# A third, short Strassen step over k-tiles 8 and 9 of the gate/up chunk pairs, separate weight rings and sums, and a later split of p

## The chip, the cores and the metric

The kernel runs on one core of a Trainium2 chip. The metric is the time of one execution on the device in microseconds, the median of several. The engines are called as the profile calls them: PE (TensorE matmul) and PEld (its weight loads), DVE (VectorE), ACT (ScalarE), POOL (GpSimd), SP (SyncE, which issues the DMAs).

## The reference

One decoder layer on 256 tokens of width 2048, all in fp32: a half-step feed-forward network (FFN), a mixer (a gated short convolution and a gated linear recurrence), a second half-step FFN, and a gated embedding. The part that matters here is the FFN, which occurs twice with weights of 2048 x 11008 and 5504 x 2048:

```python
def swiglu(x, w_in, w_out):
    a, u = jnp.split(x @ w_in, 2, axis=-1)
    return (jax.nn.silu(a) * u) @ w_out

x = layer_norm(ALPHA * x + 0.5 * swiglu(x, ffn1_w_in[i], ffn1_w_out[i]), ln_g[i, 0], ln_b[i, 0])
...
x = layer_norm(ALPHA * x + 0.5 * swiglu(x, ffn2_w_in[i], ffn2_w_out[i]), ln_g[i, 2], ln_b[i, 2])
ple = jax.nn.sigmoid(x @ ple_w_gate[i]) * (p[i] @ ple_w_proj[i])
x = layer_norm(ALPHA * x + ple, ln_g[i, 3], ln_b[i, 3])
```

## The kernel before

**Products.** The 256 tokens are two token tiles of 128 (`t` = 0, 1). Each matrix product takes a 128 x 128 block of x as the stationary operand and 512 columns of a weight row block as the moving one. To keep fp32 accuracy, each operand is split into a high part (fp32r, a cast) and a low part (what the cast lost), and each product is three matmuls, high x high, high x low, low x high (`passes`, L962 to L964). A k-tile is 128 rows of the contracted dimension; the FFN's input product has 16.

**Weight pieces.** The whole kernel works through one list of weight pieces (`plan`). A piece is usually two k-tiles by 512 columns: 128 x 1024 numbers in SBUF. For each, SP issues a load into a buffer (`weight_dma`, L868), ScalarE casts it to the high part `wh` (`weight_cast`, L897), VectorE subtracts to get the low part `wl` (`weight_split`, L908), and then PE uses it. There are six `wh`/`wl` pairs in the FFN's main ring (`NMAIN`), and four `raw` load buffers (`NRAW`). When PE's program has passed the last use of a piece, `consumed` makes its pair free, and `feed` issues what can be issued: loads first, then a cast, then a split. Two pieces at most are cast ahead of the split.

**Ticks.** Work that belongs beside the matmuls (transposes, layer norm pieces, operand splits) is put off by a number of ticks (`defer`); a tick passes with each pair of k-tiles on PE (`tick`).

**Chunk pairs.** Each FFN has 11 column chunks of its hidden width. From the third on (nine chunks per FFN) a gate chunk and an up chunk are computed together in a `Quad`. With the two token tiles as the rows of a 2 x 2 block matrix and gate and up as the columns of another, two groups of k-tiles, "low" and "high", form a 2 x 2 by 2 x 2 product. Strassen's scheme (in Winograd's form) needs 7 products for it in place of 8, and sums of the weights (t1 to t4) and of the operands (s1 to s4). Before, k-tiles 0 to 3 are low and 4 to 7 are high: two steps of two low and two high k-tiles each. K-tiles 8 to 15 are plain: four pieces of gate (a) and four of up (u), each used for both token tiles; the up pieces use the difference d of the token tiles for one of them. The seven sums of products are accumulated in seven PSUM banks, p1 to p7, and combined on VectorE by nine instructions per quad (`after`, recorded at L425, the silu ones on ScalarE at L447 and L453).

The order of pieces in a step is "11 u0 t1 u1 22 t3 a0 t2 a1 21 t4", with 11, 12, 21 and 22 the four weight blocks of the step. These blocks are loaded into five shared buffers `sraw` (`NSRAW`), in the order 12, 22, 21, 11; each buffer is reused in turn. A weight sum is an in-place VectorE addition just ahead of the cast (L891). The same five buffers first hold the fp32 operands that the sums s1 to s4 and d are made of (`sums`), in six deferred tasks when chunk 1 begins.

**Units around it.** Each quad is followed by two units of the output product of the part before (`out_unit`, 8 k-tiles each), whose results VectorE adds to x (L485). In the second FFN, x of the layer norm before it gets its gain and offset late (`affine_rows`, L359 to L365), through `raw` buffers.

**p.** The 256 columns of p are loaded at the start (`small_loads`), transposed, split into high and low, and held to the end, where a short product uses them.

## Time and profile before

| | us |
|---|---|
| median of 3 runs (2227.93 to 2230.04) | 2228.63 |
| the profiled execution, its own time | 2228.56 |
| its span, first to last instruction | 2226.70 |

The granted clock of the profiled execution was 0.997 on average. In the rows of the profile a group has its line, engine, operation, output and inputs, form and count, then its busy time in us, the mean of one in ns, and the engine's idle time before it with what ended it. Rows of the timeline have start and duration in us. Records of matmuls overlap: a matmul's duration is longer than the step to the next one. The first FFN takes about the first 700 us, the mixer and the merge the next 700, the second FFN the next 700, and the gated embedding the rest.

### The profile page before, as it was taken

Reading aid. Unit: us, or ns where it says so; the run is one execution under the profiler, and the core shown is the slowest. Engines: PE = TensorE matmul, PEld = TensorE weight load, DVE = VectorE, ACT = ScalarE, POOL = GpSimd, SP = SyncE. Lnnn points to the kernel's source line nnn. Section 1 sums busy time; section 2 is a strip of 40 time slices with the busy share of each in tenths; the row PEclk is TensorE's granted clock in tenths of the full one; section 3 lists DMA queues with packets and bytes.
Section 4 is the critical chain, followed back from the end, with each engine's and each line's share of the span. In section 5 each row is a group of like instructions: output and inputs, shape, how many; then the busy total and the mean of one; then the engine's idle time right before and its main releaser. Section 6 shows DMA issues by size and latency. Waiting matters only on the chain.

```text
span 2226.7 us, 26935 instructions
## 1 busy us (share of the span) xinstructions
PE 2203.0 (99%) x10110; PEld 1837.0 (82%) x10110; DVE 1685.6 (76%) x1952; ACT 1127.8 (51%) x1324; POOL 10.0 (0%) x32
## 2 busy tenths in 40 slices
PE   9999999999999999999999999999999999999997
PEld 7988888888887888888888888798888888888876
DVE  6788888888885678557555875769888888888668
ACT  5555555555555534434444443645555555555463
POOL 1000000000000000000000000000000000000000
PEclk9999999999999999999999999999999999999999
DMA  7666676566653665554555665567666556666564
GB/s 255 215 204 194 198 217 202 183 192 190 207 194 128 194 200 172 174 167 152 189 190 189 199 194 192 181 200 226 209 214 197 181 185 214 200 191 192 172 218 151
DMA packets 225334, 429.98 MB, mean 193 GB/s; under 512 B 13740, under 2 KB 22452, under 8 KB 225204
## 3 DMA queue, kind: packets, MB, share of 16 engines
q1 hardware_dynamic: 225204, 428.27, 60.6%
q8 instruction: 79, 1.29, 0.2%
q14 instruction: 51, 0.42, 0.1%
HBM read 426.12 MB, written 2.10 MB: 192 GB/s over the span
## 4 chain that ended last, share of the span: by engine, by line
PE 92%; DVE 4%; DMA 2%; ACT 1%; issue 1%; SPq 0%; DVEq 0%; ACTq 0%
PE bank L962 30%; PE bank L964 29%; PE bank L963 29%; DVE wl L908 2%; PE bank L243 2%; PE bank L600 1%; DVE sraw L891 1%; DMA raw<-in_ffn_w_in_dram 1%; ACT wh L897 0%; DMA sraw<-in_ffn_w_in_dram 0%; DMA gb<-in_ln_g_dram 0%; DMA x<-in_x_dram 0%; DMA raw<-in_ffn_w_out_dram 0%; DVE x L400 0%; DVE x L401 0%
## 5 line engine op out<-in xcount | busy, mean ns | idle before, releaser
L908 DVE TENSOR_TENSOR wl<-raw,wh 128x1024 fp32r<-128x1024 f32 (+2 forms) x660 | 788.6, 1203 | 262.8 <-ACT wh L897 245.4
L897 ACT CAST wh<-raw 128x1024 fp32r<-128x1024 f32 (+2 forms) x660 | 680.4, 1035 | 581.5 <-PE bank L964 410.1
L964 PE MATMUL bank<-wh,xl 128*128 128x512 f32 (+1 forms) x1736 | 670.9, 387 | 0.7 <-DVE xl L254 0.7
L963 PE MATMUL bank<-wl,xh 128*128 128x512 f32 (+1 forms) x1736 | 671.0, 387 | 0.0
L962 PE MATMUL bank<-wh,xh 128*128 128x512 f32 (+1 forms) x1736 | 669.6, 388 | 1.3 <-ACT xh L253 0.9
L897 ACT CAST wh<-sraw 128x1024 fp32r<-128x1024 f32 x252 | 262.5, 1050 | 273.1 <-PE bank L964 120.3
L908 DVE TENSOR_TENSOR wl<-sraw,wh 128x1024 fp32r<-128x1024 f32 x252 | 306.1, 1223 | 102.5 <-ACT wh L897 98.8
L964 PEld LDWEIGHTS bank<-wh,xl 128*128 128x128 f32 x1736 | 327.0, 188 | 64.5 <-DVE xl L254 2.4
L962 PEld LDWEIGHTS bank<-wh,xh 128*128 128x128 f32 x1736 | 327.1, 188 | 63.9 <-ACT xh L253 1.7
L963 PEld LDWEIGHTS bank<-wl,xh 128*128 128x128 f32 x1736 | 327.0, 188 | 61.8 <-DVE wl L908 0.2
L963 PE MATMUL bank<-wl,gh 128*128 128x512 f32 x880 | 343.9, 391 | 0.0
L964 PE MATMUL bank<-wh,gl 128*128 128x512 f32 x880 | 342.9, 391 | 0.0
L962 PE MATMUL bank<-wh,gh 128*128 128x512 f32 x880 | 341.9, 392 | 0.0
L964 PEld LDWEIGHTS bank<-wh,gl 128*128 128x128 f32 x880 | 165.4, 188 | 34.1
L962 PEld LDWEIGHTS bank<-wh,gh 128*128 128x128 f32 x880 | 165.3, 188 | 33.8
L963 PEld LDWEIGHTS bank<-wl,gh 128*128 128x128 f32 x880 | 165.4, 188 | 33.4
L891 DVE TENSOR_TENSOR sraw<-sraw 128x1024 f32<-128x1024 f32 x144 | 175.8, 1221 | 0.7
L964 PE MATMUL bank<-wh,sl 128*128 128x512 f32 x432 | 168.5, 390 | 0.0
L963 PE MATMUL bank<-wl,sh 128*128 128x512 f32 x432 | 168.4, 390 | 0.0
L962 PE MATMUL bank<-wh,sh 128*128 128x512 f32 x432 | 164.9, 390 | 0.5 <-ACT wh L897 0.5
L962 PEld LDWEIGHTS bank<-wh,sh 128*128 128x128 f32 x432 | 81.1, 188 | 17.9 <-ACT wh L897 1.4
L963 PEld LDWEIGHTS bank<-wl,sh 128*128 128x128 f32 x432 | 81.1, 188 | 16.9
(181 smaller groups left out, 1145.8 us busy)
## 6 DMA issues: line engine op xcount, KB each, us to landing
raw<-in_ffn_w_in_dram SPq DMA_DIRECT2D x176, 512.0 KB, 4.5
raw<-in_mix_w_in_dram SPq DMA_DIRECT2D x176, 512.0 KB, 4.6
raw<-in_ffn_w_out_dram SPq DMA_DIRECT2D x168, 512.0 KB, 4.9
sraw<-in_ffn_w_in_dram SPq DMA_DIRECT2D x144, 512.0 KB, 4.7
raw<-in_mix_w_out_dram SPq DMA_DIRECT2D x32, 512.0 KB, 5.4
raw<-in_ple_w_gate_dram SPq DMA_DIRECT2D x32, 512.0 KB, 4.9
raw<-in_ffn_w_in_dram SPq DMA_DIRECT2D x32, 384.0 KB, 4.0
raw<-in_branch_w_conv_dram SPq DMA_DIRECT2D x16, 512.0 KB, 4.9
```

Of the source, the lines that this page charges most:

```text
L243: state["turned"] = nc.tensor.transpose(tp[:, i * P : (i + 1) * P], src[:, i * P : (i + 1) * P], ident).ins
L600: nc.tensor.matmul(gp[:, (h * 2 + t) * 64 : (h * 2 + t + 1) * 64], kd[:, h, t * P : (t + 1) * P], qd[:, h, t, :], start=True, stop=True)
L891: nc.vector.tensor_tensor(out=raw[:, :n, :w], in0=raw[:, :n, :w], in1=raws[el["add"]][:, :n, :w], op=ALU.add)
L897: nc.scalar.copy(h[:, :n, :w], raw[:, :n, :w])
L908: nc.vector.tensor_tensor(out=l[:, :n, :w], in0=raw[:, :n, :w], in1=h[:, :n, :w].bitcast(F32), op=ALU.subtract)
L962: nc.tensor.matmul(acc, sh, wh[:, a, :n], start=first, stop=False)
L963: nc.tensor.matmul(acc, sh, wl[:, a, :n], start=False, stop=False)
L964: nc.tensor.matmul(acc, sl, wh[:, a, :n], start=False, stop=last)
```

## The change

- K-tiles 8 and 9 become a short Strassen step of one low and one high k-tile, four pieces (h1 to h4) at the head of the quad. The tile `one` holds the step's blocks 11 and 22, the tile `three` its blocks 12 and 21, each loaded in two halves. h1 is `one`; h2 is `one` plus a repeated block 12, written to a buffer of ring "12" (t1 and t3); h3 is t2 and block 21; h4 is t4, half a piece. K-tiles 10 to 15 remain plain: three a and three u pieces. A quad has 24 pieces where it had 22.
- The short step's operand sums are made of the third chunk of operands, in `short_sums` and `made_short`; with a marker task there are ten deferred tasks where there were six, and the low sums are formed in one task.
- The five shared buffers become four rings with their own counts (`HIGH`): two for "11", one each for "12", "21", "22". A quad's ring "12" takes loads only once its h2 is made. `feed` tries the rings in a fixed order, ahead of `raw`.
- A weight sum is issued by itself (`weight_add`), ahead of casts, once what it overwrites has been split (`behind`), up to one piece ahead of the split.
- The accumulators are combined as they are complete, no longer by the name of the piece; the instructions are the same.
- p is loaded, transposed and split when the last output units of the second FFN begin (`p_operand`).

The diff's core, without blank lines and without the functions whose content only moved:

```diff
+HIGH = {"11": 2, "12": 1, "21": 1, "22": 1}
...
-NSRAW = 5
...
+    STEPS = (((0, 1), (4, 5)), ((2, 3), (6, 7)))
+    SHORT = (8, 9)
+    PLAIN = ((10, 11), (12, 13), (14, 15))
+    ORDER = ("h1 u0 h2 h3 a0 h4 11.0 u1 t1.0 22.0 t3.0 a1 t2.0 21.0 t4.0 "
+             "11.1 u2 t1.1 22.1 t3.1 a2 t2.1 21.1 t4.1").split()
     def __init__(self, stat, w, cols, width, after):
         self.stat, self.w, self.cols, self.width, self.after = stat, w, cols, width, after
-        self.els = []
-        for s in range(2):
-            lo, hi = (2 * s, 2 * s + 1), (4 + 2 * s, 5 + 2 * s)
-            n0, n1 = (8 + 4 * s, 9 + 4 * s), (10 + 4 * s, 11 + 4 * s)
+        self.shorted = False
+        made = {}
+        for s, (lo, hi) in enumerate(self.STEPS):
+            sums = (2 * s, 2 * s + 1)
             k11, k12, k21, k22 = ((self, s, n) for n in ("11", "12", "21", "22"))
             step = {
-                "11": dict(src=k11, use=[("p1", 0, lo)]),
-                "t1": dict(src=k11, add=k12, use=[("p5", "s1", lo)]),
-                "22": dict(src=k22, use=[("p3", "s4", lo)]),
-                "t3": dict(src=k12, add=k22, use=[("p7", "s3", lo)], free=[k12]),
-                "t2": dict(src=k11, add=k22, use=[("p6", "s2", lo)], drop=[k22]),
+                "11": dict(src=k11, use=[("p1", 0, lo)], load=[(k11, lo, 0), (k22, hi, 1), (k12, lo, 1), (k21, hi, 0)]),
+                "t1": dict(src=k11, add=(k11, k12), behind="11", use=[("p5", "s1", sums)]),
+                "22": dict(src=k22, use=[("p3", "s4", sums)]),
+                "t3": dict(src=k12, add=(k12, k22), behind="t1", use=[("p7", "s3", sums)], free=[k12]),
+                "t2": dict(src=k11, add=(k11, k22), behind="t1 22", use=[("p6", "s2", sums)], drop=[k22]),
                 "21": dict(src=k21, use=[("p2", 0, hi)]),
-                "t4": dict(src=k11, add=k21, use=[("p4", 1, hi)], drop=[k21], free=[k11]),
+                "t4": dict(src=k11, add=(k11, k21), behind="t2 21", use=[("p4", 1, hi)], drop=[k21], free=[k11]),
             }
-            for n, ks in (("a0", n0), ("a1", n1)):
-                step[n] = dict(load=[(ks, 0)], use=[("p2", 0, ks), ("p4", 1, ks)])
-            for n, ks in (("u0", n0), ("u1", n1)):
-                step[n] = dict(load=[(ks, 1)], use=[("p3", "d", ks), ("p5", 1, ks)])
-            step["11"]["sums"] = [(k12, lo, 1), (k22, hi, 1), (k21, hi, 0), (k11, lo, 0)]
-            order = "11 u0 t1 u1 22 t3 a0 t2 a1 21 t4".split()
-            for n in order:
-                self.els.append(dict(step[n], name=n, step=s))
+            for n, el in step.items():
+                if "behind" in el:
+                    el["behind"] = max(self.ORDER.index(f"{m}.{s}") for m in el["behind"].split())
+                made[f"{n}.{s}"] = el
+        lo, hi = self.SHORT
+        one, two, three = (self, "h", "11"), (self, "h", "12"), (self, "h", "21")
+        made["h1"] = dict(src=one, use=[("p1", 0, (lo,)), ("p3", "s4", (4,))],
+                          load=[(one, (lo,), 0), (one, (hi,), 1), (three, (lo,), 1), (three, (hi,), 0)])
+        made["h2"] = dict(src=two, add=(one, three), short="h2", behind=-1, free=[two],
+                          use=[("p5", "s1", (4,)), ("p7", "s3", (4,))])
+        made["h3"] = dict(src=three, add=(two, one), short="h3", behind=self.ORDER.index("h1"), drop=[one],
+                          use=[("p6", "s2", (4,)), ("p2", 0, (hi,))])
+        made["h4"] = dict(src=three, add=(three, three), short="h4", behind=self.ORDER.index("h3"), free=[three],
+                          n=1, use=[("p4", 1, (hi,))])
+        for i, ks in enumerate(self.PLAIN):
+            made[f"a{i}"] = dict(load=[(None, ks, 0)], use=[("p2", 0, ks), ("p4", 1, ks)])
+            made[f"u{i}"] = dict(load=[(None, ks, 1)], use=[("p3", "d", ks), ("p5", 1, ks)])
+        self.els = [made[n] for n in self.ORDER]
...
+    def high(part, name):
+        return region["high"].tile([P, KG, CC], F32, tag="b" + part, name=name, bufs=HIGH[part])
...
+        def four(x11, x12, x21, x22, s1, s2, s3, s4):
+            both(s3, x11, x21, ALU.subtract)
+            both(s1, x21, x22, ALU.subtract)
+            both(s2, s1, x11, ALU.subtract)
+            both(s4, x12, s2, ALU.add)
...
+        short = spare[:, 1, :]
+        def short_sums():
+            y = [hi[t][:, 0, i * P : (i + 1) * P] for t in range(NT) for i in range(2)]
+            four(*y, *(short[:, i * P : (i + 1) * P] for i in range(4)))
+        def made_short():
+            halves(stat, "short", 0, short, 4, "s")
+            h, l = stat.parts["short", 0]
+            for i in range(4):
+                stat.parts[f"s{i + 1}", 1] = h[:, i : i + 1, :], l[:, i : i + 1, :]
         def delta(c):
+            d = hi[0][:, c % 2, :]
+            both(d, d, hi[1][:, c % 2, :], ALU.subtract)
+            halves(stat, "d", c, d, 4, "s")
+        todo = (low_sums, lambda: made("s1", x[2]), lambda: made("s2", x[0]), lambda: made("s3", s3),
+                lambda: made("s4", x[1]), short_sums, made_short, lambda: delta(2), lambda: delta(3),
+                lambda: held.update(on=True))
+        for i, fn in enumerate(todo):
...
+                after = deque([(("p1",), first), (("p3", "p5"), second), (("p6", "p7"), third),
+                               (("p2",), fourth), (("p4",), fifth)])
...
+    def p_operand():
+        for t in range(NT):
+            pin = st.tile([P, CC], F32, tag="h", name="pin", bufs=3)
+            nc.sync.dma_start(pin[:, :256], p[0, 0, t * P : (t + 1) * P, :])
+            defer(8 + t, lambda t=t, pin=pin: to_stat(pst, t, 0, pin, 2, "g"))
...
+            base = len(plan)
             for el in u.els:
-                for key, ks, n in el.get("sums", ()):
-                    loads["sraw"].append((key, kind, u.w, ks[0] * P, 2, u.cols[n], u.width))
-                if "load" in el:
-                    (ks, n), = el["load"]
-                    el["src"] = len(plan)
-                    el["free"] = [len(plan)]
-                    loads["raw"].append((len(plan), kind, u.w, ks[0] * P, 2, u.cols[n], u.width))
-                plan.append(dict(el, n=2, w=u.width, where="main"))
+                if "add" in el:
+                    adds.append(len(plan))
+                    el["behind"] += base
+                for key, ks, n in el.get("load", ()):
+                    ring = key[2] if key else "raw"
+                    if not key:
+                        key = el["src"] = len(plan)
+                        el["free"] = [key]
+                    loads[ring].append((key, kind, u.w, ks[0] * P, len(ks), u.cols[n], u.width))
+                plan.append(dict(dict(n=2, w=u.width, where="main"), **el))
...
     def weight_dma(ring="raw"):
         key, _, w, r0, n, col, width = loads[ring].popleft()
+        at = 0
         if ring == "raw":
             raw = rp.tile([P, KG, CC], F32, tag="raw", name="raw", bufs=NRAW)
             used["raw"] += 1
+        elif key in half:
+            raw, at = half.pop(key), 1
         else:
-            raw = high("sraw")
+            raw = high(ring, "raw" + ring)
+            held[ring] += 1
+            if n == 1:
+                half[key] = raw
         src = w[r0 : r0 + n * P, col : col + width].rearrange("(a p) c -> p a c", p=P)
-        nc.sync.dma_start(raw[:, :n, :width], src)
-        raws[key] = raw
+        nc.sync.dma_start(raw[:, at : at + n, :width], src)
+        if key not in half:
+            raws[key] = raw
...
+        key, kind = loads[ring][0][:2]
+        if ring == "12" and not key[0].shorted:
+            return False
+        return kind == region["kind"] and held["on"] and (held[ring] < HIGH[ring] or key in half)
...
+    def weight_add():
+        el = plan[adds.popleft()]
+        a, b = (raws[key] for key in el["add"])
+        short = el.get("short")
+        if short == "h2":
+            out = raws[el["src"]] = high("12", "raw12")
+            held["12"] += 1
+            el["src"][0].shorted = True
+            b = b[:, 0:1, :].to_broadcast([P, 2, CC])
+        elif short == "h3":
+            out, a, b = raws[el["src"]][:, 0, :], a[:, 0, :], b[:, 1, :]
+        elif short == "h4":
+            out = a = a[:, 0, :]
+            b = b[:, 1, :]
+        else:
+            out = a
+        nc.vector.tensor_tensor(out=out, in0=a, in1=b, op=ALU.add)
+        drop(el.get("drop", ()))
+        el["added"] = True
+    def addable():
+        if not adds:
+            return False
+        i = adds[0]
+        el = plan[i]
+        if i > cur["split"] + 1 or cur["split"] <= el["behind"] or any(key not in raws for key in el["add"]):
+            return False
+        return el.get("short") != "h2" or held["12"] < HIGH["12"]
...
-        if "add" in el:
-            nc.vector.tensor_tensor(out=raw[:, :n, :w], in0=raw[:, :n, :w], in1=raws[el["add"]][:, :n, :w], op=ALU.add)
-            drop(el.get("drop", ()))
...
     def feed():
         while True:
-            if may_load("sraw"):
-                weight_dma("sraw")
-            elif may_load("raw"):
-                weight_dma()
+            ring = next((r for r in ("11", "22", "12", "21", "raw") if may_load(r)), None)
+            if ring:
+                weight_dma(ring)
+            elif addable():
+                weight_add()
             elif castable():
                 weight_cast()
...
-            for bank, t, ks in el["use"]:
+            for i, (bank, t, ks) in enumerate(el["use"]):
                 tick()
                 first = bank not in ps
                 if first:
                     ps[bank] = ptile("a", bank)
                 for a, k in enumerate(ks):
                     left[bank] -= 1
-                    passes(ps[bank], u.stat, t, k, gi, a, first and a == 0, left[bank] == 0)
+                    passes(ps[bank], u.stat, t, k, gi, a if len(ks) > 1 else i, first and a == 0, left[bank] == 0)
             consumed(gi)
-            u.after(el, ps)
+            while u.after and all(b in left and not left[b] for b in u.after[0][0]):
+                u.after.popleft()[1](ps)
...
```

More of the change, by code (lines that the diff above doesn't have):

```diff
@@ L289, in sums @@
     def sums(stat):
-        x1, x2, d = plain[0, 0], plain[1, 0], high("s3")
-        x11, x12, x21, x22, s3 = x1[:, 0, :], x1[:, 1, :], x2[:, 0, :], x2[:, 1, :], d[:, 0, :]
-        s1, s2, s4 = x21, x11, x12
-        def made(key, g, src):
-            halves(stat, key, g, src, 4, "s")
-        def third():
-            difference(x11, x21, s3)
-            made("s3", 0, s3)
-        def first():
-            difference(x21, x22, s1)
-            made("s1", 0, s1)
-        def second():
-            difference(s1, x11, s2)
-            made("s2", 0, s2)
@@ L309, in fourth, with both @@
-        def fourth():
-            nc.vector.tensor_tensor(out=s4, in0=x12, in1=s2, op=ALU.add)
-            made("s4", 0, s4)
-        def delta(c):
-            a = plain[0, 1][:, c % 2, :]
-            difference(a, plain[1, 1][:, c % 2, :], a)
-            made("d", c, a)
-            if c == 3:
-                held["freed"] += 5
-        for i, fn in enumerate((third, first, second, fourth, lambda: delta(2), lambda: delta(3))):
+        def both(o, a, b, op):
+            nc.vector.tensor_tensor(out=o, in0=a, in1=b, op=op)
@@ new lines, in four, with low_sums @@
+        def four(x11, x12, x21, x22, s1, s2, s3, s4):
[3 more added lines that the diff above has]
+            both(s4, x12, s2, ALU.add)
+        lo, hi, spare = [plain[t, 0] for t in range(NT)], [plain[t, 1] for t in range(NT)], high("11", "s")
+        x = [lo[0][:, 0, :], lo[0][:, 1, :], lo[1][:, 0, :], lo[1][:, 1, :]]
+        s3 = spare[:, 0, :]
+        def low_sums():
+            four(*x, x[2], x[0], s3, x[1])
@@ new lines, in first, with second, third @@
+                def first(ps):
+                    made["c11"] = work("h")
+                    nc.scalar.copy(made["c11"], ps["p1"])
+                def second(ps):
+                    c = made["c12"] = work("silu")
+                    nc.scalar.copy(c, ps["p3"])
+                    both(c, c, ps["p5"], ALU.add)
+                def third(ps):
+                    e = made["e"] = work("silu")
+                    made["c22"] = work("h")
+                    both(e, made["c11"], ps["p6"], ALU.add)
+                    both(made["c12"], made["c12"], e, ALU.subtract)
+                    both(e, e, ps["p7"], ALU.add)
+                    both(made["c22"], ps["p5"], e, ALU.subtract)
@@ L523, in small_loads @@
         nc.sync.dma_start(normw, hg_norm_w.broadcast_to([P, P]))
-        pin = [st.tile([P, CC], F32, tag="h", name="pin", bufs=3) for t in range(NT)]
-        for t in range(NT):
-            nc.sync.dma_start(pin[t][:, :256], p[0, 0, t * P : (t + 1) * P, :])
         def place():
@@ L531, in place @@
             nc.vector.tensor_copy(gbT, tp[:, :96])
[L532 to L542 removed]
+        defer(8, place)
+    pst = Stat()
+    def p_operand():
[3 more added lines that the diff above has]
+            defer(8 + t, lambda t=t, pin=pin: to_stat(pst, t, 0, pin, 2, "g"))
     def small_inputs():
@@ L832, in hybrid_layer @@
     plan = []
-    loads = {"raw": deque(), "sraw": deque()}
+    adds = deque()
+    loads = {ring: deque() for ring in ("raw", *HIGH)}
     for u in units:
@@ L854, in hybrid_layer @@
                 plan.append(dict(src=i, free=[i], n=len(ks), w=u.width, where=where))
-    raws, pairs = {}, {}
+    raws, pairs, half = {}, {}, {}
     cur = {"cast": 0, "split": 0}
-    used = {"raw": 0, "sraw": 0}
+    used = {"raw": 0}
     room = dict(EXTRA, main=NMAIN)
@@ L875, in may_load @@
             return used["raw"] < NRAW
-        return loads[ring][0][1] == region["kind"] and 5 <= held["freed"] and held["sraw"] - held["freed"] < NSRAW
+        key, kind = loads[ring][0][:2]
+        if ring == "12" and not key[0].shorted:
+            return False
+        return kind == region["kind"] and held["on"] and (held[ring] < HIGH[ring] or key in half)
     def drop(keys):
@@ L916, in castable @@
         el = plan[i]
-        return (el["src"] in raws and el.get("add", el["src"]) in raws and room[el["where"]]
+        return (el["src"] in raws and ("add" not in el or el.get("added")) and room[el["where"]]
                 and el["where"] in ("main", region["kind"]))
```

68 lines of the change are left out of this document (19 added, 49 removed).

## The prediction

> **What bounds the kernel now.** I read the engine totals first, then the chain that ended last.
>
> ```profile
> span 2226.7 us, 26935 instructions
> PE 2203.0 (99%) x10110; PEld 1837.0 (82%) x10110; DVE 1685.6 (76%) x1952; ACT 1127.8 (51%) x1324; POOL 10.0 (0%) x32
> ...
> PE 92%; DVE 4%; DMA 2%; ACT 1%; issue 1%; SPq 0%; DVEq 0%; ACTq 0%
> ```
>
> PE is busy almost always and carries 92% of the chain. Since matmul records overlap, I check in the timeline of PE whether they follow each other at an even step. These are the first and the last of 26 wide matmuls:
>
> ```profile
> 500.10 0.39 PE L962 MATMUL bank<-wh,xh 128*128 128x512 f32 x1
> ...
> 505.77 0.39 PE L963 MATMUL bank<-wl,xh 128*128 128x512 f32 x1
> ```
>
> 25 steps in 5.67 us are 0.2268 us each. This is the price of a matmul on the path, not the 0.39 us of its record. Second, I ask whether PE waits anywhere in the chunk pairs ("quads" below). The view of waits from 1490 to 1610 us, the stretch where VectorE is latest, has one line for PE:
>
> ```profile
> PE bank L962 <- ACT wh L897: 0.5, 2, 0.3
> ```
>
> So PE sets the time in the quads, and fewer matmuls are worth their step each. The question is how near VectorE is behind it. One quad with its two out units, by windows (PE, PEld, DVE, ACT, POOL busy, clock, DMA share, GB/s):
>
> ```profile
> 1683.00:1746.50 63.50, 63.50 (x285) 52.61 (x284) 53.67 (x53) 34.20 (x36) 0.00 (x0) 1.00 0.64 199
> ```
>
> VectorE is busy for 53.67 of 63.50 us, 85%, at full clock. That is close enough for the added sums to matter.
>
> **What is removed: matmuls.** A "product" is one k-tile for one token tile or sum, three matmuls (high x high, high x low, low x high). Before, a quad has two steps of 7 x 2 products and 8 plain pieces of 4: 28 + 32 = 60 products, 180 matmuls. After, it has the two steps (28), a short step (h1, h2 and h3 of 2 products, h4 of 1: 7) and 6 plain pieces (24): 59 products, 177 matmuls. Nine quads in each of two FFNs: 18 x 3 = 54 matmuls, 54 x 0.2268 = **-12.25 us**. All are on PE's path.
>
> The Trainium skill ("TensorE: Matmul & The Clock Gate", Part 1) gives 215.7 ns from start to start for 512 columns at the full clock. By that the saving would be an estimated 11.65 us; the trace has 226.8 ns at granted clock 1.00, so the measured step stands.
>
> **What is added: VectorE work.** Its step, from these rows of the timeline:
>
> ```profile
> 1700.00 1.23 DVE L908 TENSOR_TENSOR wl<-sraw,wh 128x1024 fp32r<-128x1024 f32 x1 [3.56 <-ACT wh L897]
> 1701.14 1.22 DVE L908 TENSOR_TENSOR wl<-raw,wh 128x1024 fp32r<-128x1024 f32 x1
> ...
> 1720.83 0.68 DVE L425 TENSOR_TENSOR silu<-h,bank 128x512 f32<-128x512 f32 x1
> 1721.43 1.22 DVE L908 TENSOR_TENSOR wl<-raw,wh 128x1024 fp32r<-128x1024 f32 x1
> ```
>
> Instructions begin 1.14 us after a wide one and 0.60 us after one of 512 columns. Before, the weights of a quad cost 22 splits and 8 adds: 30 x 1.14 = 34.20 us. After: 23 whole splits and h4's half, 26.82; 9 whole adds (h2's is new) and two of 512 columns (h3, h4), 11.46; together 38.28 us, **+4.08 us per quad**. The epilogue has the same nine instructions, after the same pieces. h2's add reads a repeated operand; nearest are a product with a repeated operand and a sum without, and they cost the same, so I charge nothing extra:
>
> ```profile
> L694 DVE TENSOR_TENSOR sg<-sg,normw 128x512 f32<-128x512 f32 x4 | 2.8, 688 | 7.5 <-ACT sg L692 7.5
> L365 DVE TENSOR_TENSOR x<-x,gb 128x512 f32<-128x512 f32 x24 | 15.6, 687 | 1.1 <-DMA gb<-in_ln_b_dram 1.1
> ```
>
> If the repetition doubled it, each quad would have 1.14 us more. ScalarE gains 1.5 casts per quad and is busy 34.20 of 63.50 us: free.
>
> **What pays for it: a DMA wait.** The five shared sraw buffers give step 1's "11" no buffer until step 0 releases one. VectorE (1700.00 above, idle 3.56 us) waits for a cast, and the cast for the load:
>
> ```profile
> 1698.92 1.05 ACT L897 CAST wh<-sraw 128x1024 fp32r<-128x1024 f32 x1 [3.74 <-DMA sraw<-in_ffn_w_in_dram]
> ...
> ACT wh L897 <- DMA sraw<-in_ffn_w_in_dram: 68.7, 16, 4.8
> ...
> 1510.78 4.57 DMA sraw<-in_ffn_w_in_dram
> ```
>
> 68.7 us in 16 waits are 4.29 us, about one per quad; the last row is one on the chain. After, ring "11" has two buffers: the short step's tile is dropped at h3's add, so 11.1 loads some ten pieces before its use. The wait goes. VectorE's time through a quad's weights was 34.20 + 4.29 = 38.49 us and becomes 38.28 us: the same. What could be late next is 12.0, since ring "12" has one buffer, which holds h2's sum until h2's split. Then VectorE still has h3 (0.60 + 1.14), a0 (1.14), h4 (0.60 + 0.60), 11.0 and u1 (2 x 1.14) ahead of the add that needs 12.0: 6.36 us, against this landing:
>
> ```profile
> sraw<-in_ffn_w_in_dram SPq DMA_DIRECT2D x144, 512.0 KB, 4.7
> ...
> gb<-in_ln_b_dram SPq DMA_DIRECT2D x16, 256.0 KB, 5.3
> ```
>
> The two half loads for each short tile (256 KB, four per quad in place of two whole loads, SP's only extra issues) land in 5.3 us or less; they are issued a quad's out units ahead. I take 0 for both.
>
> **How much VectorE may be late.** Each quad's tightest piece is t1 of step 1, right behind that wait. The end of its split against PE's first use of the low part (L963), in quad 4 of the first FFN, and quads 5, 2 and 3 of the second:
>
> ```profile
> 235.92 1.23 DVE L908 TENSOR_TENSOR wl<-sraw,wh 128x1024 fp32r<-128x1024 f32 x1
> 239.57 0.39 PE L963 MATMUL bank<-wl,sh 128*128 128x512 f32 x1
> ...
> 1704.69 1.23 DVE L908 TENSOR_TENSOR wl<-sraw,wh 128x1024 fp32r<-128x1024 f32 x1
> 1709.30 0.39 PE L963 MATMUL bank<-wl,sh 128*128 128x512 f32 x1
> ...
> 1521.22 1.23 DVE L908 TENSOR_TENSOR wl<-sraw,wh 128x1024 fp32r<-128x1024 f32 x1
> 1522.95 0.39 PE L963 MATMUL bank<-wl,sh 128*128 128x512 f32 x1
> ...
> 1583.53 1.22 DVE L908 TENSOR_TENSOR wl<-sraw,wh 128x1024 fp32r<-128x1024 f32 x1
> 1584.83 0.47 PE L963 MATMUL bank<-wl,sh 128*128 128x512 f32 x1
> ```
>
> Slack: 2.42, 3.38, 0.50 and 0.08 us. The first two stand for the 16 settled quads, the last two are the tight ones behind the layer norm. After, a quad takes PE 3 x 0.2268 = 0.68 us less and VectorE 0.21 us less, so slack shrinks by 0.47 us plus any wait W that is left. With W = 0 the settled quads keep 1.9 us or more: cost 0. The tight two would lose 0 and 0.39 us: +0.4.
>
> **The rest.** Each FFN forms short sums: four VectorE sums of 128 columns and one more 512-column cast and split. Nearest to the small sums is
>
> ```profile
> L726 DVE SCALAR_TENSOR_TENSOR cT<-uT,cw,cT 128x128 f32<-128x128 f32 x32 | 9.4, 349 | 0.0
> ...
> 1479.83 1.29 DVE L364 TENSOR_TENSOR x<-x,gb 128x512 f32<-128x512 f32 x2 [3.82 <-DMA gb<-in_ln_g_dram]
> ```
>
> which bounds them: 4 x 0.35 + 0.60 = 2.0 us, and 0 if hidden. In the second FFN they come shortly before an idle of 3.82 us on VectorE, which would absorb them; if that cover is gone, 2.0. I take +0.3. The weight rings open eight ticks later (19, not 11, of the 32 in chunk 1's units), still 13 ticks ahead of q2: 0. The seven accumulators are opened within 12 products (8.2 us), not 20. The last bank of the out units is read by VectorE after quad 6 has begun:
>
> ```profile
> 1747.91 0.39 PE L962 MATMUL bank<-wh,xh 128*128 128x512 f32 x1
> ...
> 1749.93 0.68 DVE L485 TENSOR_TENSOR x<-x,bank 128x512 f32<-128x512 f32 x1
> ```
>
> 1749.93 + 0.68 - 1747.91 = 2.7 us, in time for 8.2: 0. The p rows move from the start to the last out units: the same two loads, four transposes (0.8 us of records), casts and splits. At the start they may give back up to 0.8 us; at the end the out units need VectorE little. Their loads stand in SP's queue behind "h" buffers, ahead of weight loads with time in hand. I take 0.
>
> **Sum**, against the profiled execution's own 2228.56 us (span 2226.7; the three runs have median 2228.63): 2228.56 - 12.25 + 0.4 + 0.3 = **2217.0 us**. Its own range: down to 2214 (the 0.5 us of PE waits and p's 0.8 gone, 2215.0, and a run's scatter of 1), up to 2220 (short sums bare, both tight quads 0.5 late).
>
> **Rivals.**
> - **Slower: 12.0 comes late.** If VectorE's order puts t1.0's add right behind h2's split, nothing covers the load, and a wait W stays in every quad. A settled quad stalls by W + 0.47 - 2.9 (middle of 2.42 and 3.38), a tight one by W + 0.47 - 0.3. It decides from W = 2.8, where 18 W - 38.5 eats the 12.25 us; at 4.29 it costs 38.7: 2255 us. For it: one buffer, and 1.7 us of margin. Against: 6.36 us of other work in between. Chance 0.10.
> - **VectorE already sets the pace.** Then 18 x 4.08 = 73.4 us are added, 68.7 us of waits go, the matmuls count nothing: 2233.3 us. The even step of PE and the slack speak against it. The Trainium skill ("Perfetto Trace Analysis", Identifying the Most-Contended Engine) would rank this way: matmul busy is no measure, weight loads and VectorE occupancy are. In the windows row these are 83% and 85%, so VectorE leads by that rule. Chance 0.05.
> - **No change: the tight quads pay in full.** If in q2 and q3 of the second FFN another load (raw, gb) takes the place of the wait that goes, both lose 4.08, and the short sums 2.0: 10.2 us back, 2226.5 us. For it: slack 0.08 and the idle for gb. Against: the waits on the chain there are sraw's. Chance 0.13.
>
> **How the numbers follow.** The forecast has 0.72, all of it faster by more than 0.2% (4.5 us, about what a measurement of this kernel can tell from no change: below 2224.1). The third rival is the "same" case, 0.13. The first two are slower, 0.15. The range 2214 to 2228 holds the forecast and the third rival with a run's scatter, 0.85.
>
> **What would show it.** PE should have 54 instructions fewer (10056), with the same step. DVE should rise by about 18 x 4.08 + 4 = 77 us. The casts' wait for loads of "11" should vanish, and no wait for a "12" load above 2.8 us appear; PE's waits between 1490 and 1610 us should stay about 1 us. The forecast is wrong if PE's busy share falls in the quads, or if VectorE idles in front of the t adds.

## The result and the profile after

The changed kernel is slower: a median of 2233.86 us (2233.20 to 2236.82) against 2228.62 us (2227.02 to 2230.04), a ratio of 1.0026 [1.0016, 1.0036]. The prediction, 2217.0 us with a range up to 2228, missed by 16.9 us, and on the wrong side.

The totals of the profile after, and the engines' shares of its chain:

```profile
span 2232.4 us, 27107 instructions
...
PE 2198.4 (98%) x10056; PEld 1828.0 (82%) x10056; DVE 1761.9 (79%) x2052; ACT 1158.5 (52%) x1361; POOL 10.1 (0%) x32
...
PE 91%; DVE 5%; issue 1%; DMA 1%; ACT 1%; SPq 0%; DVEq 0%; ACTq 0%
```

The planned sizes are all there: 54 matmuls fewer, and VectorE busy for 76.3 us more (77 predicted). The span is 5.7 us longer all the same. To see where, I took all rows of PE's timeline and summed, from each matmul's start to the next, what exceeds its step (0.2268 us for 512 columns, in proportion for fewer). Below, such an excess is called a gap; a slow clock counts in it too. Some 700 matmuls of 128 columns and fewer have steps of about 0.11 us, so the totals depend on how these are counted. Strictly in proportion the whole kernels have 76.7 and 94.6 us; with 0.06 us as the least step, and without excesses under 0.05 us, they have 44.3 and 61.5, near the table's totals. Differences between kernels and the rows for the quads agree within 1.3 us in all these counts.

| gaps of PE, us | before | after |
|---|---|---|
| whole kernel | 46.2 | 63.3 |
| 100 to 160 us (quad 2, first FFN) | 0.3 | 4.4 |
| 1490 to 1620 us (quads 2 and 3, second FFN) | 1.7 | 14.5 |
| the rest | 44.2 | 44.4 |

So 12.25 us of matmuls went as planned, and 17.1 us of gaps came, nearly all of them in three of the 18 quads, the first ones of each FFN. The other 15 have no single gap above 0.3 us. The waits of PE after, first from 120 to 140 us, then from 1490 to 1610 us (us in total, times, longest):

```profile
PE bank L1030 <- DVE wl L974: 2.0, 1, 2.0
```

```profile
PE bank L1030 <- DVE wl L974: 6.0, 5, 2.0
PE bank L1029 <- ACT wh L963: 1.7, 3, 0.8
```

Each time PE waits for a piece's low part or for a cast. Of the casts behind these waits, those begun at 1532.63 and 1537.77 us had themselves waited for a weight sum (line 942) of VectorE. The rest of the loss is a slow clock behind such waits. PE's timeline at the end of quad 2 of the first FFN (start, duration):

```profile
131.66 0.40 PE L1031 MATMUL bank<-wh,xl 128*128 128x512 f32 x1
134.10 0.71 PE L1030 MATMUL bank<-wl,gh 128*128 128x512 f32 x1 [2.04 <-DVE wl L974]
...
137.59 0.42 PE L1029 MATMUL bank<-wh,gh 128*128 128x512 f32 x1
```

The start at 134.10 comes 2.44 us after the one before, 2.21 us too late. Then eight steps take 3.49 us instead of 1.81, another 1.7 us. In the second FFN the same happens behind a gap as long, which ends at 1608.43 us, and behind a shorter one, which ends at 1543.98 us. The windows rows of the first and the last of these places (their last three numbers are the granted clock, the DMA share and GB/s) have a clock of 0.91, and so has that from 1600 to 1620 us:

```profile
120.00:140.00 20.00, 17.85 (x71) 13.96 (x70) 17.24 (x20) 8.79 (x11) 0.00 (x0) 0.91 0.53 165
...
1540.00:1560.00 20.00, 18.01 (x75) 14.09 (x75) 18.14 (x22) 9.50 (x12) 0.00 (x0) 0.91 0.74 235
```

Three slow stretches of about 1.7 us make some 5 of the 17.1 us.

Why was the split late? The piece is the first of the out units (stationary `gh`). VectorE's timeline at that place, after:

```profile
124.77 1.22 DVE L942 TENSOR_TENSOR raw<-raw,raw 128x1024 f32<-128x1024 f32 x1
128.75 0.69 DVE L453 TENSOR_TENSOR silu<-h,bank 128x512 f32<-128x512 f32 x1 [2.76 <-PE bank L1031]
129.35 1.22 DVE L974 TENSOR_TENSOR wl<-raw,wh 128x1024 fp32r<-128x1024 f32 x1
130.49 0.69 DVE L453 TENSOR_TENSOR silu<-silu 128x512 f32<-128x512 f32 x1
131.09 1.22 DVE L942 TENSOR_TENSOR raw<-raw,raw 128x1024 f32<-128x1024 f32 x1
132.22 0.68 DVE L453 TENSOR_TENSOR h<-h,bank 128x512 f32<-128x512 f32 x1
132.82 2.36 DVE L974 TENSOR_TENSOR wl<-raw,wh 128x1024 fp32r<-128x1024 f32 x2
```

Line 942 at 124.77 is t4.1's sum. The instruction at 128.75 is the epilogue's e = c11 + p6, and it waits 2.76 us for PE to finish t2.1. The split of t4.1 (129.35) and that of the out unit's first piece (132.82) stand behind it, and so does a weight sum for the next quad (131.09). ScalarE has the casts for these splits ready one after the other from about 127.1 us on:

```profile
126.08 4.41 ACT L963 CAST wh<-raw 128x1024 fp32r<-128x1024 f32 x5 [2.18 <-DVE raw L942]
```

VectorE works in order, so for the last 1.6 us or so of its wait it idles with splits due, and PE then waits for them. The same place before, where the split of t4.1 (124.82) and those of the out units' first two pieces stand first and e needs no wait:

```profile
124.82 1.22 DVE L908 TENSOR_TENSOR wl<-sraw,wh 128x1024 fp32r<-128x1024 f32 x1
125.96 1.22 DVE L908 TENSOR_TENSOR wl<-raw,wh 128x1024 fp32r<-128x1024 f32 x1
128.35 1.23 DVE L908 TENSOR_TENSOR wl<-raw,wh 128x1024 fp32r<-128x1024 f32 x1 [1.17 <-ACT wh L897]
129.49 0.68 DVE L425 TENSOR_TENSOR silu<-h,bank 128x512 f32<-128x512 f32 x1
```

The out unit's first split began at 125.96 us there and begins at 132.82 us after.

A settled quad after (quad 5 of the first FFN) shows the good order too, with splits ahead of e and no idle time; PE has no gap there:

```profile
315.75 2.35 DVE L974 TENSOR_TENSOR wl<-raw,wh 128x1024 fp32r<-128x1024 f32 x2
318.02 0.69 DVE L942 TENSOR_TENSOR raw<-raw,raw 128x512 f32<-128x512 f32 x1
318.62 0.68 DVE L453 TENSOR_TENSOR silu<-h,bank 128x512 f32<-128x512 f32 x1
```

The Trainium skill ("TensorE: Matmul & The Clock Gate", the engine queue depths under Architectural detail) calls VectorE's queue strictly first in, first out; the rows at 128.75 and 129.35 agree.

In the second FFN there is more. VectorE's waits from 1490 to 1610 us, before and then after:

```profile
DVE wl L908 <- ACT wh L897: 12.5, 6, 4.6
DVE silu L425 <- PE bank L964: 0.4, 1, 0.4
DVE x L364 <- DMA gb<-in_ln_g_dram: 0.2, 1, 0.2
```

```profile
DVE wl L974 <- ACT wh L963: 5.5, 7, 1.6
DVE x L392 <- DMA gb<-in_ln_g_dram: 4.8, 3, 1.7
DVE silu L453 <- PE bank L1031: 2.6, 2, 2.4
DVE h L498 <- PE bank L1031: 0.5, 1, 0.5
```

The wait for casts fell by 7.0 us, as it should, but VectorE's idle time did not: 13.1 us before, 13.4 after. The layer norm's gain rows (`gb`) and the epilogue took its place. So in these two quads nothing paid for the added sums.

### The profile page after: what moved, and what is told of

The parts are those of the page before. It is cut to its first block, busy times and chain, and to the rows that moved or that the text cites. A ratio compares the mean times of both kernels' runs of the same rounds, so it can differ in the third digit from the quotient of the medians.

```text
span 2232.4 us, 27107 instructions
## 1 busy us (share of the span) xinstructions
PE 2198.4 (98%) x10056; PEld 1828.0 (82%) x10056; DVE 1761.9 (79%) x2052; ACT 1158.5 (52%) x1361; POOL 10.1 (0%) x32
## 4 chain that ended last, share of the span: by engine, by line
PE 91%; DVE 5%; issue 1%; DMA 1%; ACT 1%; SPq 0%; DVEq 0%; ACTq 0%
PE bank L1030 29%; PE bank L1031 29%; PE bank L1029 29%; DVE wl L974 3%; PE bank L264 2%; DVE raw L942 1%; PE bank L626 1%; ACT wh L963 1%; DMA raw<-in_ffn_w_in_dram 0%; DMA gb<-in_ln_g_dram 0%; DVE x L428 0%; DMA raw<-in_ple_w_gate_dram 0%; DVE x L429 0%; DVE silu L453 0%; PE bank L596 0%
## 5 line engine op out<-in xcount | busy, mean ns | idle before, releaser
L963 ACT CAST wh<-raw 128x1024 fp32r<-128x1024 f32 (+2 forms) x948 | 961.5, 1031 | 835.3 <-PE bank L1031 528.2
L974 DVE TENSOR_TENSOR wl<-raw,wh 128x1024 fp32r<-128x1024 f32 (+2 forms) x948 | 1115.6, 1199 | 281.5 <-ACT wh L963 261.7
L1030 PE MATMUL bank<-wl,xh 128*128 128x512 f32 (+1 forms) x1682 | 650.1, 388 | 1.0 <-DVE wl L974 0.8
L1031 PE MATMUL bank<-wh,xl 128*128 128x512 f32 (+1 forms) x1682 | 649.6, 387 | 1.0 <-DVE xl L275 1.0
L1029 PE MATMUL bank<-wh,xh 128*128 128x512 f32 (+1 forms) x1682 | 644.7, 388 | 2.0 <-ACT xh L274 1.6
L942 DVE TENSOR_TENSOR raw<-raw,raw 128x1024 f32<-128x1024 f32 (+1 forms) x180 | 210.2, 1168 | 8.9 <-DMA raw<-in_ffn_w_in_dram 7.3
L1030 PE MATMUL bank<-wl,sh 128*128 128x512 f32 x468 | 182.5, 390 | 1.9 <-DVE wl L974 1.9
L1029 PE MATMUL bank<-wh,sh 128*128 128x512 f32 x468 | 180.7, 390 | 1.4 <-ACT wh L963 1.3
L1031 PEld LDWEIGHTS bank<-wh,sl 128*128 128x128 f32 x468 | 87.8, 188 | 18.2
L516 DVE TENSOR_TENSOR x<-x,bank 128x512 f32<-128x512 f32 x64 | 43.6, 682 | 18.2 <-PE bank L1031 18.2
```

What stands on the lines that cost most here:

```text
L516: nc.vector.tensor_tensor(out=xc, in0=xc, in1=acc, op=ALU.add)
L942: nc.vector.tensor_tensor(out=out, in0=a, in1=b, op=ALU.add)
L963: nc.scalar.copy(h[:, :n, :w], raw[:, :n, :w])
L974: nc.vector.tensor_tensor(out=l[:, :n, :w], in0=raw[:, :n, :w], in1=h[:, :n, :w].bitcast(F32), op=ALU.subtract)
L1029: nc.tensor.matmul(acc, sh, wh[:, a, :n], start=first, stop=False)
L1030: nc.tensor.matmul(acc, sh, wl[:, a, :n], start=False, stop=False)
```

## The experiments

There are three theories. **Order**: the epilogue's e ahead of the splits costs the stalls, and behind them the change gains. **Work**: VectorE's 4.08 us per quad don't fit beside the layer norm's late gain and offset. **Loads**: it is the wait for the gain rows, not the work. Where the expectations below say LOAD, they mean Work; where they say WAIT or GB, they mean Loads. Unless it says otherwise, an experiment is the changed kernel with one edit; every ratio is against the kernel before, measured beside it.

**1. e behind the splits** (e_behind). The first instruction of the task for p6 and p7 is issued behind the split of the third piece after the one that PE has just done, or behind the last split issued. (`split_at` notes the split of each piece and, under "now", the piece that PE's program has just passed; the lines that fill it are left out here.)

```diff
...
-                    both(e, made["c11"], ps["p6"], ALU.add)
+                    with tc.issue_after(split_at[min(split_at["now"] + 3, cur["split"] - 1)]):
+                        both(e, made["c11"], ps["p6"], ALU.add)
...
```

> The changed kernel, with one difference: the first VectorE instruction of the accumulators' third combination (c11 + p6, which waits for PE's last matmul of t2.1) is queued behind the split of the first weight piece of the following out unit, so it cannot stand ahead of the splits of t4.1 and of that piece. Theory ORDER (the loss of the changed kernel is this instruction standing in VectorE's queue ahead of splits that PE needs first, plus the half clock after the stall): the stalls at 132 and 1606 us (2.2 us idle and about 2 us of slow matmuls each) go, and part of the one at 1540 us; time 2220 to 2226. Theory LOAD (VectorE simply has 4.08 us too much per quad behind the layer norm, whatever the order): the work is the same and so is the time, 2231 to 2236.

2225.46 us, ratio 0.9989 [0.9981, 0.9998], where the change itself has 1.0026: about 8 us gained with no arithmetic changed. All gaps went from 63.3 to 54.7 us. At the end of quad 2 of the first FFN (VectorE's timeline, then the windows row):

```profile
130.47 1.22 DVE L976 TENSOR_TENSOR wl<-raw,wh 128x1024 fp32r<-128x1024 f32 x1
131.61 0.68 DVE L454 TENSOR_TENSOR silu<-h,bank 128x512 f32<-128x512 f32 x1
```

```profile
120.00:140.00 20.00, 20.00 (x90) 16.52 (x89) 17.99 (x20) 9.63 (x11) 0.00 (x0) 1.00 0.58 183
```

PE is busy throughout and its clock is whole. In the second FFN 11.2 us of gaps stay (14.5 after the change). PE's and VectorE's waits there, from 1495 to 1610 us:

```profile
PE bank L1032 <- DVE wl L976: 4.8, 4, 2.0
PE bank L1031 <- ACT wh L965: 2.4, 5, 0.8
```

```profile
DVE wl L976 <- ACT wh L965: 5.4, 6, 1.2
DVE x L393 <- DMA gb<-in_ln_g_dram: 4.7, 3, 2.0
```

None of the three slow stretches is left. That at 1544 us had followed a gap of 1.61 us beyond the step, and e_behind has nearly the same gap there (1.44 us, ending at 1538.94) at full clock, so up to 1.7 us of the gain may be the clock's and not the order's. The order is a cause, worth some 8 us with the slow clock that follows its stalls, but not the only one.

**2. Without the short step** (two_steps). All quads as before (eight k-tiles by products), with the new rings, the separate sums and the late p kept:

```diff
+    LONG_PLAIN = ((8, 9), (10, 11), (12, 13), (14, 15))
+    LONG_ORDER = ("11.0 u0 t1.0 u1 22.0 t3.0 a0 t2.0 a1 21.0 t4.0 "
+                  "11.1 u2 t1.1 u3 22.1 t3.1 a2 t2.1 a3 21.1 t4.1").split()
...
-                units.append(Quad(xs, w_in, (c0, DFF + c0), CC, after))
+                units.append(Quad(xs, w_in, (c0, DFF + c0), CC, after, short=False))
...
```

> The changed kernel without the short step: k-tiles 8 and 9 are plain again (22 pieces and 60 products per quad), with the new rings, separate sums, late p and late combination kept. Theory LOAD: VectorE has 4.08 us less per quad and the wait for 11.1 is gone too, so no stalls in the quads; the matmuls saved are 0; time 2226 to 2229. Theory ORDER: the order at the quad's end comes from the separately issued sums and not from the short step, so stalls of about 4 us stay in one to three quads: 2231 to 2240.

2226.30 us, ratio 0.9994 [0.9986, 1.0003], with 43.7 us of gaps and none in the quads. ScalarE's waits for the loads of the FFN's input weights are one line, where before had 68.7 us for `sraw` and 25.9 us for `raw` (the first row is of before, the second of the changed kernel, the last of this run):

```profile
ACT wh L897 <- DMA raw<-in_ffn_w_in_dram: 25.9, 20, 4.5
...
ACT wh L963 <- DMA raw<-in_ffn_w_in_dram: 16.7, 14, 5.0
...
ACT wh L975 <- DMA raw<-in_ffn_w_in_dram: 23.1, 19, 4.9
```

So the rings alone take most of the wait away, and by themselves gain nothing: before, PE hardly waited in the quads (0.5 us from 1490 to 1610 us). The loss comes only with the short step. This run also has the sums as issues of their own, and at the end of quad 2 of the first FFN e stands behind the splits all the same (VectorE's timeline):

```profile
125.89 1.23 DVE L986 TENSOR_TENSOR wl<-raw,wh 128x1024 fp32r<-128x1024 f32 x1 [1.12 <-ACT wh L975]
127.04 0.68 DVE L465 TENSOR_TENSOR silu<-h,bank 128x512 f32<-128x512 f32 x1
```

So separate sums by themselves don't bring e to the front. Theory ORDER had expected that of this run, and there it was wrong.

**3. Without the short step where it stalled** (mixed). As 2, but only in quad 2 of the first FFN and quads 2 and 3 of the second:

```diff
...
+                units.append(Quad(xs, w_in, (c0, DFF + c0), CC, after, short=ch > (3 if ln_i else 2)))
...
```

> The changed kernel with the short step left out in the quads that stalled alone: quad 2 of the first FFN, quads 2 and 3 of the second (45 matmuls saved in the other 15 quads, 10.2 us). Theory LOAD: the stalls go with the 4.08 us of VectorE work per quad: 2217 to 2222. Theory ORDER: the queue's order in these quads decides, and it may stay as it is: 2225 to 2234.

2222.96 us, ratio 0.9981 [0.9972, 0.9990]. The three places are free of gaps, but the stall moved on: in quad 3 of the first FFN, which had had none, VectorE shows

```profile
191.28 0.69 DVE L465 TENSOR_TENSOR silu<-h,bank 128x512 f32<-128x512 f32 x1 [2.65 <-PE bank L1043]
191.89 1.22 DVE L986 TENSOR_TENSOR wl<-raw,wh 128x1024 fp32r<-128x1024 f32 x1
```

and PE a gap of 2.21 us behind it, likewise at 1659.74 us in quad 4 of the second. Order again: with the layer norm far away the same row stalls PE, in the first or second quad with a short step.

**4. p alone** (p_late). The kernel before, with p loaded, transposed and split in the last out units:

```diff
-        units.append(("tail" + name, lambda: None))
+        units.append(("tail" + name, p_operand if ln_i else lambda: None))
...
```

> The kernel before with p loaded and split when the last output units of the second FFN begin, and nothing else of the change. If p at the start held up the first units, 1 to 2 us are gained at the start (2226.5 to 2228); if the late p costs something behind the second FFN, up to 2 us are lost. I expect 2227.

2227.54 us, ratio 0.9998 [0.9989, 1.0008]: nothing that can be measured.

**5. Both, 1 and 3** (mixed_e).

> The short step left out in quad 2 of the first FFN and quads 2 and 3 of the second, and c11 + p6 queued behind the split of the following out unit's first piece. Theory ORDER plus LOAD (both the queue's order and the VectorE work in the first quads cost): the two stalls of 4 us that were left in the kernel without the short step in these quads go, and nothing new comes: 10.2 us of matmuls saved against before, 2216 to 2219. If the stalls only move to the next quad again, 2221 to 2224.

2216.79 us, ratio 0.9954 [0.9941, 0.9966]; gaps 44.1 us, none in the quads. With 45 matmuls fewer (10.2 us at the step), 11.3 us are gained.

**6. Gain and offset later** (e_gb). e_behind with the affine work (gain and offset) put off by 12 ticks instead of 4, so that its loads should have landed:

```diff
...
-        defer(4, apply)
+        defer(12, apply)
...
```

> c11 + p6 behind the out unit's first split, and the gain and offset of the layer norm applied 12 ticks after their loads are issued, not 4. Theory GB (what is left, about 8 us at quad 2 of the second FFN, starts with VectorE waiting for the gain rows in its queue, three times 1.5 to 2 us): these waits go; 2219 to 2223. Theory LOAD: VectorE catches up nothing, since the work is the same: 2224 to 2227.

2226.44 us, ratio 0.9991 [0.9982, 1.0000]. A miss: the wait for `gb` fell only from 4.7 to 3.5 us (1495 to 1610 us) and the gaps from 11.2 to 9.8 us, so it says nothing on a kernel without the wait.

**7. No gain and offset** (e_noaff). e_behind without the second layer norm's gain and offset: neither their eight loads (four of gain rows, four of offset rows) nor their 16 VectorE instructions. It computes other numbers.

```diff
...
+        if i == 1:
+            unsettled.remove(c)
+            return
...
```

> c11 + p6 behind the out unit's first split, and the gain and offset of the second layer norm not applied to x (it leaves out four loads and sixteen VectorE instructions of 512 columns in the second FFN's first quads). Both theories: the stalls in quads 2 and 3 of the second FFN go nearly all, 2214 to 2219. If this is no better than the kernel with the later application, the waits and not the work were the cost; if it is better by 3 us or more, the work was.

2215.36 us, ratio 0.9943 [0.9931, 0.9956]; gaps of 0.5 us where e_behind has 11.2. Work and loads together are the rest of the loss, about 10 us.

**8. No early sums** (e_adds). e_behind with each weight sum queued behind the last split issued, to see whether the sums that run ahead do harm:

```diff
...
-        nc.vector.tensor_tensor(out=out, in0=a, in1=b, op=ALU.add)
+        with tc.issue_after(split_at[cur["split"] - 1]):
+            nc.vector.tensor_tensor(out=out, in0=a, in1=b, op=ALU.add)
...
```

> c11 + p6 behind the out unit's first split, and every weight sum queued behind the last split issued before it, so that the next quad's h2 cannot stand ahead of the out unit's splits. Theory EARLY SUMS (separately issued sums run ahead in VectorE's queue and wait there for their loads, 0.4 to 0.6 us, plus 1.14 us of work that PE doesn't need yet): the slack at each out unit's first piece rises from 1.6 us to 3 us or more, and the two stalls of 1.4 us in front of it go; 2221 to 2224. If the order of the sums doesn't matter: 2225 to 2227. If the sums come too late now, casts wait for them: above 2227.

2260.12 us, ratio 1.0149 [1.0133, 1.0164]. The casts' waits for sums, in this run and then in e_behind:

```profile
ACT wh L966 <- DVE raw L945: 310.9, 153, 4.2
```

```profile
ACT wh L965 <- DVE raw L944: 99.3, 70, 3.8
```

Sums held back like this come too late, at a cost of some 35 us against e_behind. Whether some of them run too far ahead in e_behind, this run can't say.

**9. Short step left out only behind the layer norm** (best2). e_behind, and the quad of experiment 2 in quads 2 and 3 of the second FFN alone:

```diff
...
+                units.append(Quad(xs, w_in, (c0, DFF + c0), CC, after, short=ln_i == 0 or ch > 3))
...
```

> c11 + p6 behind the out unit's first split, and the short step left out in quads 2 and 3 of the second FFN alone (quad 2 of the first FFN has it again): three matmuls fewer than the kernel that left it out in three quads, 0.7 us. If the queue's order was the whole cost in the first FFN (theory ORDER): 2215 to 2217. If VectorE's work costs there too (theory LOAD): 2218 to 2220.

2215.62 us (2214.33 to 2216.03), ratio 0.9944 [0.9932, 0.9957]: faster than both kernels, and the lowest median of all versions with the whole computation (the interval of mixed_e overlaps with its own).

```profile
span 2212.5 us, 27077 instructions
...
PE 2188.7 (99%) x10062; PEld 1826.2 (83%) x10062; DVE 1752.7 (79%) x2042; ACT 1154.2 (52%) x1357; POOL 10.0 (0%) x32
```

VectorE has 67.1 us more than before and PE no stall in the quads. In the first FFN all nine quads have the short step here, and none has a stall, so order was all that its quad 2 lost.

**10. Gain and offset on GpSimd** (e_affpool). e_behind with these 16 instructions moved off VectorE:

```diff
...
-                nc.vector.tensor_tensor(out=xc, in0=xc, in1=gb[:, 0, :], op=ALU.mult)
-                nc.vector.tensor_tensor(out=xc, in0=xc, in1=gb[:, 1, :], op=ALU.add)
+                on = nc.gpsimd if i == 1 else nc.vector
+                on.tensor_tensor(out=xc, in0=xc, in1=gb[:, 0, :], op=ALU.mult)
+                on.tensor_tensor(out=xc, in0=xc, in1=gb[:, 1, :], op=ALU.add)
...
```

> c11 + p6 behind the out unit's first split, the short step in all 18 quads, and the gain and offset of the second layer norm applied by GpSimd instead of VectorE (16 instructions of 512 columns moved, none left out). Theory LOAD: VectorE has as little to do in quads 2 and 3 of the second FFN as when they were left out, so 2214 to 2217. Rival: GpSimd is so slow, or slows VectorE so much, that an out unit or a split waits for it: 2222 to 2232.

2226.17 us, ratio 0.9996 [0.9987, 1.0005]: nothing gained. The timeline of both engines shows a reason:

```profile
1522.82 4.50 POOL L394 TENSOR_TENSOR x<-x,gb 128x512 f32<-128x512 f32 x2 [17.29 <-DVE wl L977]
1527.29 4.48 POOL L395 TENSOR_TENSOR x<-x,gb 128x512 f32<-128x512 f32 x2
```

```profile
1523.86 9.00 DVE L977 TENSOR_TENSOR wl<-raw,wh 128x1024 fp32r<-128x1024 f32 x4
```

While GpSimd multiplies and adds, four splits take 9.00 us, 2.25 us each instead of 1.14.

**11. The work without its loads** (e_const). e_behind; in place of gain and offset x is multiplied twice by rows that lie in SBUF, so the 16 instructions remain and the loads go:

```diff
...
+                    nc.vector.tensor_tensor(out=xv, in0=xv, in1=row, op=ALU.mult)
+                    nc.vector.tensor_tensor(out=xv, in0=xv, in1=row, op=ALU.mult)
...
```

> c11 + p6 behind the out unit's first split, and in the second FFN x is multiplied twice by a row block that lies in SBUF (normw, repeated), in place of being scaled by the loaded gain and added the loaded offset: the same sixteen VectorE instructions at the same ticks, but no loads, no raw buffer taken and nothing to wait for (it computes other numbers). Theory WORK (VectorE's sixteen instructions on top of the short step's 4.08 us per quad are what the two quads can't hold): 2222 to 2226. Theory WAIT (the three waits of 1.5 to 2 us for the gain rows, which came in place of the wait for 11.1): 2214 to 2218.

2222.78 us, ratio 0.9978 [0.9968, 0.9987], but not an answer. With no load to wait for, the instructions were issued earlier and ran inside the layer norm:

```profile
1427.76 1.29 DVE L399 TENSOR_TENSOR x<-x,normw 128x512 f32<-128x512 f32 x2 [4.55 <-PE bank L265]
```

The gaps from 1400 to 1440 us doubled from 7.1 to 14.2 us (some 1.8 us of it slow clock: 0.91 from 1420 to 1440 us), and those in quads 2 and 3 were gone. It moved the work instead of freeing it of its loads.

**12. The same, in its old place** (e_const_late). As 11, each pair behind the last split issued before it:

```diff
...
+                    with tc.issue_after(split_at[cur["split"] - 1]):
...
```

> As the run before (sixteen VectorE instructions of 512 columns on x with a row block that lies in SBUF, no loads, no raw buffer, nothing to wait for; it computes other numbers), but each group queued behind the last split issued before it, so that they stay in quads 2 and 3 of the second FFN and don't run ahead into the layer norm. Theory WORK (VectorE has more work there than the quads hold): stalls of 6 us or more stay between 1500 and 1610 us, 2222 to 2226. Theory WAIT (the waits for the gain rows in VectorE's queue were the cost): hardly a stall there, 2214 to 2218.

2223.18 us, ratio 0.9976 [0.9967, 0.9985]. The work stood from 1468 to 1553 us, no wait for `gb` was left, and the gaps from 1490 to 1620 us were 7.6 us. PE's waits from 1495 to 1610 us:

```profile
PE bank L1042 <- DVE wl L986: 2.8, 3, 1.3
PE bank L1041 <- ACT wh L975: 1.2, 4, 0.4
```

Of the 10.7 us of gaps between e_behind (11.2) and e_noaff (0.5), 3.6 go with the loads and 7.1 stay with the work: a third and two thirds. The times say the same (0.9989, 0.9976, 0.9943), but the first two intervals overlap, so the shares are rough.

## Why the prediction was wrong

- **The matmuls** (-12.25 us): right. 54 fewer at an unchanged step: the work of all matmuls is 2150.1 us before and 2137.8 after. e_noaff, where the new gaps are gone, is 12.7 us faster than before.
- **VectorE's sum** (+4.08 us per quad, 77 in all): right, 76.3. Had the repeated operand doubled h2's sum, it would be some 20 us more.
- **The wait for block 11.1 goes, no 12.0 comes late** (the first rival): right. Waits for loads of the FFN's input weights fell from 94.6 us (68.7 + 25.9) to 16.7 us on ScalarE, and no weight sum waited more than 1.3 us for a load.
- **Settled quads, p and banks** at 0, short sums at 0.3: right as far as it can be seen. 15 of 18 quads have no stall, and where the short sums of the second FFN are made (1400 to 1490 us) the gaps are 6.9 us before and 7.3 after.
- **"The epilogue has the same nine instructions, after the same pieces."** This is the step that failed first. It is true of the pieces and of the work, and I priced it at 0; but the price of an instruction in an in-order queue is also what stands behind it. Before, t4.1's split and two more stood ahead of e. In the first quads with the short step e came ahead of t4.1's split, VectorE idled up to 2.76 us for a bank while splits came due, and PE lost 2.2 us and then 1.7 us at the slow clock. e_behind prices it at about 8 us, slow clock included. The slack was read at t1 of step 1 alone, but the long stalls came at the out unit's first piece (`gh`). A test close to it stood in the prediction (VectorE idling in front of the t sums), but I applied it only to loads.
- **"The tight two would lose 0 and 0.39 us: +0.4."** Mis-sized: with the order mended they still have 11.2 us of gaps (1.7 before). The sum 38.49 to 38.28 let the vanishing wait pay for the added work. But there VectorE's idle time stayed as it was (13.1 and 13.4 us): the wait for `gb` took the place. That is the third rival, and its price is near: 10.2 us back, 2226.5 us, against 2225.46 measured for e_behind. In part that is luck, for 2.0 of the 10.2 us are short sums, which cost about 0.4. Its reason, a load, is only about a third of it. Two thirds stay when the loads are removed and go when the affine work is left out too (e_noaff), so the quads hold the 4.08 us more per quad or the affine work, but not both.
- **Together** 8.6 us of gaps for the order and 10.7 for quads 2 and 3 are 19.3; the measured 17.1 is less by some 2 us found elsewhere, 1.7 of them in the first 20 us (8.6 to 6.9), where p was. That p is the reason isn't shown: p_late, which moves p alone, can't be told from no change.
- **VectorE as the pace** (second rival): its 2233.3 us hit the measured time by chance. It would add time in every quad and count the matmuls for nothing; 15 quads show no stall, and best2 gains 12.2 us with VectorE 67.1 us busier than before. The ranking by occupancy from the Trainium skill that I set beside it ("Perfetto Trace Analysis", Identifying the Most-Contended Engine) would not have led to the three places either.

Open: what in the short step brings e to the front of the queue, and only in the first quads that have it (the order is fixed when the program is built, by what could be issued at that moment; separate sums alone don't do it, as experiment 2 shows); and whether quads 2 and 3 of the second FFN could keep the short step with the affine work in another place. e_const moved that work, but into the layer norm, where it made 7.1 us of gaps for the 11 it took from the quads; besides, it was only put off by eight ticks (e_gb).

## What to carry to other kernels

When an edit changes when instructions are issued, write out the in-order queue of the engine they share, and ask of every instruction that can wait for PE what PE will next need that stands behind it; counts and durations don't show this. A wait that goes pays for added work only where the next thing needed isn't late too, so price it in the tightest stretch and not on average. A gain spread over many equal stages can be lost in three of them: sum the gaps by place before blaming the whole change.

## What was not expected of the hardware

**A short stall can halve PE's pace for a while.** After a matmul that began 2.44 us after the one before, eight steps came to 0.44 us each (134.10 to 137.59 us); the same happened behind the gaps that end at 1608.43 and, with only 1.61 us beyond the step, at 1543.98 us, where the granted clock of 20 us is 0.91 each time. It isn't certain: in e_behind a gap of 2.27 us beyond the step is followed by one step of 0.33 us and then by steps of 0.23 to 0.24, at clock 1.00:

```profile
1523.94 0.50 PE L1032 MATMUL bank<-wl,sh 128*128 128x512 f32 x1 [2.00 <-DVE wl L976]
1524.27 0.40 PE L1033 MATMUL bank<-wh,sl 128*128 128x512 f32 x1
1524.51 0.39 PE L1031 MATMUL bank<-wh,sh 128*128 128x512 f32 x1
```

So the length of the gap alone doesn't decide it.

The Trainium skill ("TensorE: Matmul & The Clock Gate", HAM oscillation) warns of idle gaps over some 3.4 us. In Part 1 the same page of the Trainium skill says that the window in which the activity is measured is free-running and isn't reset when the kernel starts. The three gaps above are shorter than 3.4 us, so here a shorter gap was enough, if not always.

**GpSimd beside VectorE halves VectorE.** With two-operand instructions in SBUF on both, a split takes 2.25 us where it took 1.14 us, and GpSimd takes 2.25 us for 512 columns (e_affpool, 1523 to 1532 us). The Trainium skill ("SBUF — State Buffer", SBUF: two separate sides) describes a lock on a port pair, held for a whole instruction, between a VectorE instruction with two SBUF inputs and a GpSimd instruction that reads SBUF. The four and four instructions that fill the same 9 us would fit such a lock; no run here has the GpSimd instructions alone, so it isn't shown.
